# A first partition maximum on POOL, head-norm roots spread through memory, plain transposes for the first token blocks

## The chip, the cores and the metric

The kernel runs on one core of one Trainium2 chip. The metric is the time of one execution on the device in microseconds (us), as the median of several runs. One execution is also taken by the hardware profiler; its time is given beside its span, from the first to the last instruction. TensorE (PE in the rows) multiplies matrices, VectorE (DVE) and ScalarE (ACT) work on rows of 128 partitions, POOL (GpSimd) works across partitions, and SP only issues DMAs here.

## The reference

One decoder block on 1024 tokens of width 1024, in float32. Two branches run side by side, a gated linear recurrence (HGRN2, 8 heads of 128) and sliding-window attention with sinks (16 query heads of 64):

```python
xn = rms_norm(x, norm_w[l])
proj = xn @ w_in[l]
hq, hf, hi, hg, aq, ak, av, ag, mh, ma = jnp.split(proj, SPLIT_POINTS, axis=-1)
f = lb + (1.0 - lb) * sigmoid(hf);  k_h = 1.0 - f;  q_h = silu(hq);  v_h = hi
o_h = hgrn2_chunkwise(q_h, k_h, v_h, log(f))
o_h = rms_norm(o_h, hgrn_norm_w[l])          # one norm per head and token
y_h = (o_h * silu(hg)) @ w_branch_hgrn[l]
y_a = (attention(aq, ak, av, sinks) * silu(ag)) @ w_branch_attn[l]
x = x + (sigmoid(mh) * y_h + sigmoid(ma) * y_a) @ w_out[l]
return rms_norm(x, final_norm_w)
```

## The kernel before

Every product of the large matrices is made of three float16 products: weights and activations are scaled by a power of two and split into a high and a low half (hi, lo). The scale of a weight block comes from its largest absolute value: VectorE reduces along rows (line 205, in the first block line 176), POOL takes the maximum over the partitions (`all_max`, line 122), and a few small VectorE instructions make the power of two (`pow2_of`, lines 125 to 133). ScalarE writes hi, VectorE lo (lines 236 and 237; in the first block, loaded and converted in two parts, lines 194 and 199).

*The front.* `Tokens` loads the eight token blocks of 128 rows. A block's mean square is taken by ScalarE (`square`, lines 427 and 428, with a square root), and `diag` refines the inverse root in four small VectorE instructions. For blocks 0 to 3 it then writes the identity, scaled by that root, into `dg` (line 454), and `turn_x` (line 460) turns and scales a 128x128 piece by a float32 matmul with `dg`, which TensorE runs as two instructions. Blocks 4 to 7 are scaled whole (line 450) and turned by a plain transpose with the identity (line 458), one instruction a piece. `split_x` (lines 464 and 465) multiplies by the norm's gains and writes the halves xh (ScalarE) and xl (VectorE). `norm_w` arrives as 8 rows on SP's queue and is turned by TensorE with the identity (line 150); its maximum (line 344) gives the scale of x. The identity comes from a POOL memset and an affine_select (masks.py:199). TensorE is kept busy beforehand by 24 transposes of the identity (line 1123). All this stands in a stretch with an order written by hand (`tc.manual_schedule`, from line 1119): there each engine's queue follows the program text. Outside it, the build's own scheduler orders each engine's instructions.

*The blocks.* Each block of `seq` is 256 columns of a weight; TensorE goes through the blocks one after the other, into accumulator banks from a pool of three (`pj`). The recurrence of each head (`hgrn`) is a generator that runs in the background: `bg.step(ns)` is called after each part of a block and lets the generators run on a credit of `bg.rate` (half) of the ns that TensorE spends, each `yield cost, wait` taking `cost` from the credit and barring that head for `wait` ns. Ahead of the last head gate, `bg.drain()` emits what is left.

*The head norm.* `o` (tile kT) is a head's output with the value dimension on the partitions and 1024 tokens along the row, `k` holds its squares. TensorE sums the squares over partitions (`ms`, line 681), so that the mean squares, and after `rsqrt` the inverse roots `rs`, stand as 128 partitions by 8 columns: token t of chunk c at partition t, column c. They are needed along the row and equal on all partitions. Two groups of four float32 matmuls (`rb`, line 690) with the identity spread them, and VectorE multiplies each half of `o` by them (line 694).

Of the kernel before, what the change touches and what calls it, by code (L numbers as in the profile page):

```python
# [14 lines left out]
F32 = mybir.dt.float32  # L15
# [4 lines left out]
ALU = mybir.AluOpType  # L20
# [3 lines left out]
P = 128  # L24
# [43 lines left out]
def hybrid_block(ctx: ExitStack, tc: _tile.TileContext, x, norm_w, w_in, hlb, hnw, wbh, sinks, wba, w_out, fnw, out):  # L68
# [9 lines left out]

    uid = [0]
# [55 lines left out]

    ident = const.tile([P, P], F32, name="ident")
# [4 lines left out]
    nwr = slot("nwr", [KT, P])  # L141
    SP.dma_start(nwr[:], norm_w[0].rearrange("(k p) -> k p", p=P))
# [5 lines left out]
    def turn_rows(src, n):  # L148
        ps = bank("vT")
        PE.transpose(ps[:, 0:n], src[:], ident[0:n, 0:n])  # L150
        return ps
# [190 lines left out]
    def norm_max():  # L342
        nmx = small("nmx", 1)
        V.tensor_reduce(nmx[:], nw[:], axis=AX.X, op=ALU.max, apply_absolute_value=True)
        return all_max(nmx[:])

    def norm_scale(top):
        sx, sxi = pow2_of(top, 10)
        yield
        V.tensor_copy(sxi_c[:], sxi[:])  # L350
        V.tensor_scalar(nws[:], nw[:], sx[:], None, ALU.mult)
# [62 lines left out]
    class Tokens:  # L414
# [22 lines left out]
        def diag(self, scaled=False):  # L437
            r, h = self.r, self.h
            V.reciprocal(r[:], r[:])
            if self.by_act:  # L440
                V.tensor_scalar(h[:], self.m[:], EPS, -0.5, ALU.add, ALU.mult)
            else:
                V.tensor_scalar(h[:], self.m[:], -0.5, None, ALU.mult)
            yield
            V.scalar_tensor_tensor(h[:], r[:], h[:], r[:], ALU.mult, ALU.mult)
            yield
            V.scalar_tensor_tensor(r[:], h[:], 1.5, r[:], ALU.add, ALU.mult)
            yield
            if scaled:
                V.tensor_scalar(self.x[:], self.x[:], r[:], None, ALU.mult)  # L450
                self.dg = None
                return
            self.dg = slot("dg", [P, P])
            V.tensor_scalar(self.dg[:], ident[:], r[:], None, ALU.mult)

    def turn_x(ps, tok, j, k):
        if tok.dg is None:
            PE.transpose(ps[:, j * P : (j + 1) * P], tok.x[:, k * P : (k + 1) * P], ident[:])
            return
        PE.matmul(ps[:, j * P : (j + 1) * P], tok.x[:, k * P : (k + 1) * P], tok.dg[:], start=True, stop=True)  # L460
# [74 lines left out]
    def hgrn(h):  # L535
# [148 lines left out]
        rsqrt(rs[:], rm[:], NB)  # L684
        yield 1800, 8000
        for b in range(2):
            rb = bank("rb")
            for j in range(4):
                p = 4 * b + j
                PE.matmul(  # L690
                    rb[:, j * P : (j + 1) * P], rs[:, p : p + 1].broadcast_to([P, P]), ident[:], start=True, stop=True
                )
            sli = slice(b * HALF, (b + 1) * HALF)
            V.tensor_tensor(o[:, sli], o[:, sli], rb[:], ALU.mult)
            if b == 0:
                yield 900, 0
# [422 lines left out]
    with tc.manual_schedule(engines=MANUAL):  # L1119
        A.activation(small("tab", 1)[:], eps[:], AF.Sqrt)  # L1120
        warm = bank("warm", pj)
        for i in range(WARM):
            PE.transpose(warm[:, 0:P], ident[:], ident[:])
            if i == 3:
                V.tensor_copy(nw[:], turn_rows(nwr, KT)[:, 0:KT])
# [20 lines left out]
        in_turn(norm_scale(top))  # L1146
        first.max_part(0)
        tok[0].square(True)
        tok[1].square(True)
        first.scale_part(0)  # L1150
        first.hi_part(0, 0)
        in_turn(tok[0].diag())
        tok[2].square(True)
        in_turn(tok[1].diag())
# [3 lines left out]
        in_turn(tok[2].diag())  # L1158
        in_turn(tok[3].diag())
# [26 lines left out]
        bounds = turn_rows(vecs, 3 * KT)  # L1186
# [10 lines left out]
        in_turn(tok[4].diag(True), tok[5].diag(True))  # L1197
        in_turn(tok[6].diag(True), tok[7].diag(True))
# [142 lines left out]
```

## Time and profile before

| | before |
|---|---|
| median of 3 runs | 1202.01 us (1199.67 to 1202.31) |
| the profiled execution | 1200.46 us |
| its span | 1198.8 us |
| TensorE (PE) busy | 1150.4 us (96%) |
| VectorE (DVE) busy | 860.6 us (72%) |
| ScalarE (ACT) busy | 527.1 us (44%) |
| POOL busy | 46.3 us (4%) |
| DMA, mean | 69 GB/s |
| TensorE clock granted, mean | 0.991 |

The page's 40 slices of 30 us show TensorE at three tenths in the first slice, and at nine tenths or more in nearly all that follow, so the busy share of the whole says little of the front. A busy TensorE is not one at its peak. In a timeline row, "x8" means eight instructions that were merged; the start is that of the first. [...]

### The profile page before, as it was taken

To read this page: it belongs to the slowest core of one execution; us is meant where nothing else is said; L and a number is where in the kernel's file an instruction comes from. 1 tells how busy PE (TensorE), PEld (TensorE's weight loads), DVE (VectorE), ACT (ScalarE), POOL (GpSimd) and SP (SyncE) were. 2 spreads that over 40 slices of the span, in tenths; PEclk is the share of its full clock that TensorE was granted. 3 is DMA by queue.
4 is the path that set the end of the run, shared out by engine and by line. 5 is a ranking of instruction groups with operands and counts; after the bars stand their busy time and mean duration, and the time that the engine had idled before them with its cause. 6 is when DMAs were issued, how large, how long until landed. Compare 5 with 4: busy or idle time off the path is not lost.

```text
span 1198.8 us, 18078 instructions
## 1 busy us (share of the span) xinstructions
PE 1150.4 (96%) x7130; PEld 671.7 (56%) x7130; DVE 860.6 (72%) x2032; ACT 527.1 (44%) x1021; POOL 46.3 (4%) x96
## 2 busy tenths in 40 slices
PE   3999999999999999999999989999997999999997
PEld 3556687687688576574554544445454444444444
DVE  2887886895995996775777774259996877367645
ACT  2732532533433343353845761147778450223323
POOL 0240000000000000000000000000000000000000
PEclk8999999999999999999999999999999999999999
DMA  6121111111111111112562552124545412131312
GB/s 211 37 98 44 36 36 36 36 36 36 36 36 36 36 36 36 36 36 71 102 128 54 115 115 71 36 71 100 108 95 126 85 36 71 36 106 36 141 53 106
DMA packets 132646, 82.47 MB, mean 69 GB/s; under 512 B 81200, under 2 KB 129360, under 8 KB 132560
## 3 DMA queue, kind: packets, MB, share of 16 engines
q1 hardware_dynamic: 132560, 81.30, 24.7%
q8 instruction: 56, 0.92, 0.3%
q14 instruction: 30, 0.25, 0.1%
HBM read 57.17 MB, written 4.19 MB: 51 GB/s over the span
## 4 chain that ended last, share of the span: by engine, by line
PE 76%; DVE 10%; ACT 6%; DMA 5%; issue 2%; SPq 0%; POOL 0%; DVEq 0%; POOLq 0%; ACTq 0%
PE pm L303 19%; PE pg L303 11%; PE pv L315 7%; PE po L1282 7%; PE pq L303 7%; PE pf L303 5%; PE paq L303 5%; PE lv L613 3%; DMA pT<-ph 3%; ACT sp L816 2%; PE pk L303 2%; DVE ph L827 2%; DMA aot<-ohl 2%; PE pf L1129 1%; DVE sp L806 1%
## 5 line engine op out<-in xcount | busy, mean ns | idle before, releaser
L303 PEld LDWEIGHTS <-wh 128*128 128x128 f16 x2304 | 224.1, 98 | 256.9 <-issue 5.5
L303 PEld LDWEIGHTS <-wl 128*128 128x128 f16 x1152 | 112.7, 98 | 130.2
L236 ACT ACTIVATE wh<-raw,p_s 128x512 f16<-128x512 f32 x164 | 104.6, 709 | 117.3 <-issue 42.7
L237 DVE SCALAR_TENSOR_TENSOR wl<-raw,p_s,wh 128x512 f16<-128x512 f32 x164 | 114.1, 748 | 45.1 <-PE pm L303 18.6
L205 DVE TENSOR_REDUCE wmx<-raw 128x1 f32<-128x2048 f32 x45 | 102.6, 2281 | 47.0 <-DMA raw<-in_w_in_dram 25.2
L303 PE MATMUL pm<-hl,wh 128*128 128x512 f16 x512 | 117.0, 379 | 0.0
L1282 PE MATMUL po<-wo,hl 128*128 128x512 f16 (+1 forms) x408 | 83.1, 367 | 0.0
L816 ACT ACTIVATE sp<-sp,anm 128x256 f32<-128x256 f32 (+1 forms) x128 | 61.7, 483 | 24.5 <-DVE anm L811 24.0
L315 PEld LDWEIGHTS <-xh 128*128 128x128 f16 x640 | 62.7, 98 | 7.7
L1282 PEld LDWEIGHTS <-hl 128*128 128x128 f16 x408 | 39.9, 98 | 43.2
L303 PE MATMUL pg<-xl,wh 128*128 128x512 f16 x256 | 62.0, 379 | 0.0
L303 PE MATMUL pg<-xh,wh 128*128 128x512 f16 x256 | 60.8, 379 | 0.9 <-DVE qs L763 0.9
L303 PE MATMUL pm<-xh,wh 128*128 128x512 f16 x256 | 61.4, 382 | 0.0
L303 PE MATMUL pm<-xl,wh 128*128 128x512 f16 x256 | 61.3, 379 | 0.0
L303 PE MATMUL pg<-xh,wl 128*128 128x512 f16 x256 | 61.1, 379 | 0.0
L303 PE MATMUL pm<-xh,wl 128*128 128x512 f16 x256 | 60.7, 379 | 0.0
L303 PE MATMUL pm<-hl,wl 128*128 128x512 f16 x256 | 60.5, 379 | 0.0
L122 POOL PARTITION_ALL_REDUCE p_r<-wmx x47 | 26.6, 570 | 872.6 <-DVE wmx L205 656.3
L806 DVE CUSTOM_DVE_ANT_0 sp<-as,amask,qsc 128x256 f32<-128x256 f32 (+1 forms) x128 | 52.4, 463 | 3.8 <-DMA pT<-ph 3.5
L497 ACT ACTIVATE sg<-pg,wc 128x512 f32<-128x512 f32 x32 | 21.9, 683 | 47.0 <-PE pg L303 46.9
L315 PE MATMUL pv<-wh,xl 128*128 128x256 f16 x320 | 42.0, 273 | 0.0
L315 PE MATMUL pv<-wh,xh 128*128 128x256 f16 x320 | 41.6, 273 | 0.0
(219 smaller groups left out, 1921.7 us busy)
## 6 DMA issues: line engine op xcount, KB each, us to landing
raw<-in_w_in_dram SPq DMA_DIRECT2D x33, 1024.0 KB, 5.1
xt<-in_x_dram SPq DMA_DIRECT2D x8, 512.0 KB, 6.7
raw<-in_w_branch_hgrn_dram SPq DMA_DIRECT2D x4, 1024.0 KB, 5.2
raw<-in_w_branch_attn_dram SPq DMA_DIRECT2D x4, 1024.0 KB, 5.9
raw<-in_w_out_dram SPq DMA_DIRECT2D x4, 1024.0 KB, 5.1
xr<-in_x_dram SPq DMA_DIRECT2D x8, 512.0 KB, 8.3
out_dram<-xr SPq DMA_DIRECT2D x8, 512.0 KB, 2.6
raw<-in_w_in_dram SPq DMA_DIRECT2D x2, 512.0 KB, 4.1
```

The costliest lines, as they stand in the source:

```text
L122: last_all_max[0] = G.partition_all_reduce(r[:], mx, channels=P, reduce_op=bass_isa.ReduceOp.max)
L205: V.tensor_reduce(mx[:, j : j + 1], self.raw[:, ks], axis=AX.XY, op=ALU.max, apply_absolute_value=True)
L236: A.activation(hi, raw, AF.Copy, scale=s[:])
L237: V.scalar_tensor_tensor(lo, raw, s[:], hi, ALU.mult, ALU.subtract)
L303: PE.matmul(ps, w[:, k, ci * P : (ci + 1) * P], act(ai, k, t0, HALF), start=(n == 0), stop=(n == 3 * KT - 1))
L315: PE.matmul(ps, act(ai, k, t0, P), w[:, k, n0 : n0 + ncol], start=(n == 0), stop=(n == 3 * KT - 1))
L497: A.activation(sg[:], ps[:], AF.Sigmoid, scale=c[:])
L613: PE.matmul(lv[:, ms], kq[:, 0, ms], kq[:, 1, ms], start=True, stop=True)
L806: V.tensor_tensor_reduce(self.s[:, i, 0:nk], self.ps[a][:, e * 256 : e * 256 + nk], amask[:, self.n % 2, 0:nk], qsc[:], NEG, ALU.add, ALU. ...
L816: A.activation(self.s[:, i, 0 : self.nk], self.s[:, i, 0 : self.nk], AF.Exp, bias=self.nm[:, i : i + 1], accum_out=self.dn[:, i : i + 1],)
L827: V.scalar_tensor_tensor(self.hl[:, 1], self.s[:, :, 0 : self.nk], 2.0**14, self.hl[:, 0], ALU.mult, ALU.subtract)
L1282: PE.matmul(ps[:, g[0] : g[1]], mact(ai, k, tb * P, P), w, start=(t == 0), stop=(t == 3 * KT - 1))
```

## The change

Three things are changed.

1. POOL's first instruction of its kind is a maximum over partitions of a column of zeros, ahead of the identity's affine_select; nobody reads the result. `norm_w` is loaded by ScalarE's queue into 8 rows of a tile of 128 rows that VectorE has cleared, and its maximum is taken from there. The turn of `norm_w` moves behind the scaling of token block 0, and the copy out of it into `norm_scale`, which moves behind the first weight part's scale. TensorE's 24 opening instructions become float32 matmuls on a tile of ones.
2. In `hgrn`, the roots `rs` are written by a POOL DMA to 1024 floats in device memory and read back by a second one, broadcast to all 128 partitions, into the tile `k`. One VectorE multiply over 1024 columns, whose second operand steps by 8, replaces two from accumulator banks. The `rb` matmuls are gone. The generator yields once more, 900 of cost.
3. Token blocks 0 to 3 are scaled whole by VectorE and turned by plain transposes, as blocks 4 to 7 were; the scaling of blocks 0 and 1 moves ahead of the weight scale.

```diff
--- before.py
+++ after.py
@@ -76,6 +76,9 @@
     pj = ctx.enter_context(tc.tile_pool(name="pj", bufs=3, space=PSUM))
     sm = ctx.enter_context(tc.tile_pool(name="sm", bufs=5, space=PSUM))
 
+    dr = ctx.enter_context(tc.tile_pool(name="dr", bufs=2, space=bass.MemoryType.DRAM))
+    BQ = nc.gpsimd
+
     uid = [0]
 
     def nm(s):
@@ -133,13 +136,19 @@
         return s, inv
 
 
+    zero = const.tile([P, 1], F32, name="zero")
+    G.memset(zero[:], 0.0)
+    all_max(zero[:])
     ident = const.tile([P, P], F32, name="ident")
     make_identity(nc, ident[:])
     ones = const.tile([P, 1], F32, name="ones")
     G.memset(ones[:], 1.0)
 
-    nwr = slot("nwr", [KT, P])
-    SP.dma_start(nwr[:], norm_w[0].rearrange("(k p) -> k p", p=P))
+    nwr = slot("nwr", [P, P])
+    V.memset(nwr[:], 0.0)
+    A.dma_start(nwr[0:KT, :], norm_w[0].rearrange("(k p) -> k p", p=P))
+    wsrc = slot("wsrc", [P, P])
+    V.memset(wsrc[:], 1.0)
     vecs = slot("vecs", [3 * KT, P])
     nw = const.tile([P, KT], F32, name="nw")
     cols = const.tile([P, 3 * KT], F32, name="cols")
@@ -147,7 +156,7 @@
 
     def turn_rows(src, n):
         ps = bank("vT")
-        PE.transpose(ps[:, 0:n], src[:], ident[0:n, 0:n])
+        PE.transpose(ps[:, 0:n], src, ident[0:n, 0:n])
         return ps
 
 
@@ -341,12 +350,12 @@
 
     def norm_max():
         nmx = small("nmx", 1)
-        V.tensor_reduce(nmx[:], nw[:], axis=AX.X, op=ALU.max, apply_absolute_value=True)
+        V.tensor_reduce(nmx[:], nwr[:], axis=AX.X, op=ALU.max, apply_absolute_value=True)
         return all_max(nmx[:])
 
-    def norm_scale(top):
+    def norm_scale(top, turned):
         sx, sxi = pow2_of(top, 10)
-        yield
+        V.tensor_copy(nw[:], turned[:, 0:KT])
         V.tensor_copy(sxi_c[:], sxi[:])
         V.tensor_scalar(nws[:], nw[:], sx[:], None, ALU.mult)
 
@@ -434,7 +443,7 @@
         def root(self):
             A.activation(self.r[:], self.m[:], AF.Sqrt)
 
-        def diag(self, scaled=False):
+        def scale(self):
             r, h = self.r, self.h
             V.reciprocal(r[:], r[:])
             if self.by_act:
@@ -446,18 +455,10 @@
             yield
             V.scalar_tensor_tensor(r[:], h[:], 1.5, r[:], ALU.add, ALU.mult)
             yield
-            if scaled:
-                V.tensor_scalar(self.x[:], self.x[:], r[:], None, ALU.mult)
-                self.dg = None
-                return
-            self.dg = slot("dg", [P, P])
-            V.tensor_scalar(self.dg[:], ident[:], r[:], None, ALU.mult)
+            V.tensor_scalar(self.x[:], self.x[:], r[:], None, ALU.mult)
 
     def turn_x(ps, tok, j, k):
-        if tok.dg is None:
-            PE.transpose(ps[:, j * P : (j + 1) * P], tok.x[:, k * P : (k + 1) * P], ident[:])
-            return
-        PE.matmul(ps[:, j * P : (j + 1) * P], tok.x[:, k * P : (k + 1) * P], tok.dg[:], start=True, stop=True)
+        PE.transpose(ps[:, j * P : (j + 1) * P], tok.x[:, k * P : (k + 1) * P], ident[:])
 
     def split_x(half, k, ps):
         dst = slice(half * HALF, (half + 1) * HALF)
@@ -682,18 +683,17 @@
         rs, rm = small("ors", NB), small("orm", NB)
         V.tensor_scalar(rm[:], ms[:, 0:NB], EPS, None, ALU.add)
         rsqrt(rs[:], rm[:], NB)
+
+        flatrs = dr.tile([P * NB], F32, tag="rs", name=nm("rsd"))
+        BQ.dma_start(flatrs[:].rearrange("(t c) -> t c", c=NB), rs[:])
+        BQ.dma_start(k[:], flatrs[:].rearrange("(o d) -> o d", o=1).broadcast_to([P, P * NB]))
         yield 1800, 8000
-        for b in range(2):
-            rb = bank("rb")
-            for j in range(4):
-                p = 4 * b + j
-                PE.matmul(
-                    rb[:, j * P : (j + 1) * P], rs[:, p : p + 1].broadcast_to([P, P]), ident[:], start=True, stop=True
-                )
-            sli = slice(b * HALF, (b + 1) * HALF)
-            V.tensor_tensor(o[:, sli], o[:, sli], rb[:], ALU.mult)
-            if b == 0:
-                yield 900, 0
+        yield 900, 0
+        yield 900, 0
+        V.tensor_tensor(
+            o[:].rearrange("p (c t) -> p c t", c=NB), o[:].rearrange("p (c t) -> p c t", c=NB),
+            view(k, 0, [[1, NB], [NB, P]]), ALU.mult,
+        )
         ohT[h] = kT
         ohT_flat[h] = o
         yield 900, 0
@@ -1120,9 +1120,7 @@
         A.activation(small("tab", 1)[:], eps[:], AF.Sqrt)
         warm = bank("warm", pj)
         for i in range(WARM):
-            PE.transpose(warm[:, 0:P], ident[:], ident[:])
-            if i == 3:
-                V.tensor_copy(nw[:], turn_rows(nwr, KT)[:, 0:KT])
+            PE.matmul(warm[:, 0:P], wsrc[:], wsrc[:], start=True, stop=True)
 
         def mm_first(ps, i, half, n, wi, ai, k):
             w = (first.hi, first.lo)[wi]
@@ -1143,20 +1141,21 @@
 
         hf_tiles(0)
         top = norm_max()
-        in_turn(norm_scale(top))
         first.max_part(0)
         tok[0].square(True)
         tok[1].square(True)
+        in_turn(tok[0].scale())
+        turned = turn_rows(nwr[0:KT], KT)
+        in_turn(tok[1].scale())
         first.scale_part(0)
         first.hi_part(0, 0)
-        in_turn(tok[0].diag())
+        norm_scale(top, turned)
         tok[2].square(True)
-        in_turn(tok[1].diag())
+        in_turn(tok[2].scale())
         first.lo_part(0, 0)
         tok[3].square(True)
         first.hi_part(0, 1)
-        in_turn(tok[2].diag())
-        in_turn(tok[3].diag())
+        in_turn(tok[3].scale())
         first.lo_part(0, 1)
         for j in range(4):
             for k in range(6):
@@ -1183,7 +1182,7 @@
         pass_first(ps0, 0, 0, range(KT), (0, 1))
         for i in range(2):
             first.outscale(i)
-        bounds = turn_rows(vecs, 3 * KT)
+        bounds = turn_rows(vecs[:], 3 * KT)
         pass_first(ps0, 0, 1, range(KT), (1, 0))
         pass_first(ps0, 0, 1, range(KT), (0, 1))
         tok[4].square(True)
@@ -1194,8 +1193,8 @@
         V.tensor_tensor(dif[:], l1, l0, ALU.subtract)
         tok[6].square(True)
         tok[7].root()
-        in_turn(tok[4].diag(True), tok[5].diag(True))
-        in_turn(tok[6].diag(True), tok[7].diag(True))
+        in_turn(tok[4].scale(), tok[5].scale())
+        in_turn(tok[6].scale(), tok[7].scale())
         setup_bounds(dif)
         n = [0, 0]
         ps1 = [bank("pf", pj), None]
```

## Rows read from the trace of the kernel before

**Rows 1.** Windows: length, busy PE, PEld, DVE, ACT, POOL, clock, DMA, GB/s.

```profile
60.00:525.00 465.00, 465.00 (x3111) 323.15 (x3110) 372.51 (x731) 175.77 (x305) 25.79 (x43) 1.00 0.13 42
```

**Rows 2.** POOL's timeline: start, duration, instruction, [idle before it, its releaser].

```profile
9.67 0.28 POOL masks.py:199 TENSOR_SCALAR_AFFINE_SELECT ident<-ident 128x128 f32<-128x128 f32 x1 [8.60 <-issue]
18.61 0.38 POOL L122 PARTITION_ALL_REDUCE p_r<-nmx  x1 [8.66 <-issue]
21.23 0.35 POOL L122 PARTITION_ALL_REDUCE p_r<-wmx  x1 [2.25 <-DVE wmx L176]
...
55.97 0.59 POOL L383 TENSOR_SCALAR_AFFINE_SELECT mk<-mk 128x128 f32<-128x128 f32 x1
...
70.55 0.36 POOL L122 PARTITION_ALL_REDUCE p_r<-wmx  x1 [0.80 <-DVE wc L247]
```

**Rows 3.** Timeline of all engines, first 37 us, same columns.

```profile
6.80 1.06 ACT L427 ACTIVATE xj<-xt 128x1024 f32<-128x1024 f32 x1 [4.52 <-DMA xt<-in_x_dram]
...
19.92 1.21 DVE L176 TENSOR_REDUCE wmx<-raw 128x1 f32<-128x1024 f32 x1
...
22.26 0.14 DVE L439 RECIPROCAL xr<-xr 128x1 f32<-128x1 f32 x1
...
22.38 0.72 ACT L194 ACTIVATE wh<-raw,p_s 128x512 f16<-128x512 f32 x1 [12.70 <-DVE p_s L132]
...
22.94 0.29 DVE L454 TENSOR_SCALAR dg<-ident,xr 128x128 f32<-128x128 f32 x1
...
23.28 7.67 PE L460 MATMUL xT<-dg,xt 128*128 128x128 f32 x48 [8.33 <-DVE dg L454]
...
24.03 0.74 DVE L199 SCALAR_TENSOR_TENSOR wl<-raw,p_s,wh 128x512 f16<-128x512 f32 x1
24.17 0.29 ACT L428 ACTIVATE xr<-xm,eps 128x1 f32<-128x1 f32 x1
...
29.86 3.58 ACT L464 ACTIVATE xh<-xT,nws 128x512 f16<-128x512 f32 x6 [3.42 <-PE xT L460]
...
36.34 1.89 PE L1129 MATMUL pf<-xh,wh 128*128 128x512 f16 x8
```

**Rows 4.** VectorE groups by form: count, busy us, mean ns, idle before.

```profile
L694 DVE TENSOR_TENSOR kT<-kT,rb 128x512 f32<-128x512 f32 x16 | 10.9, 681 | 10.2 <-PE rb L690 10.1
L570 DVE TENSOR_TENSOR k<-k,inv 128x256 f32<-128x256 f32 x16 | 10.3, 645 | 0.0
L450 DVE TENSOR_SCALAR xt<-xt,xr 128x1024 f32<-128x1024 f32 x4 | 2.8, 750 | 0.0
```

**Rows 5.** DMA issues, first 60 us: size, median us to landing.

```profile
snk<-in_attn_sinks_dram SPq DMA_DIRECT2D x1, 8.0 KB, 11.4
```

**Rows 6.** Windows of the front, columns as in rows 1.

```profile
12.00:14.00 2.00, 2.00 (x11) 2.00 (x10) 0.00 (x0) 0.00 (x0) 0.00 (x0) 1.00 1.02 403
14.00:14.50 0.50, 0.50 (x7) 0.50 (x6) 0.00 (x0) 0.00 (x0) 0.00 (x0) 1.00 1.04 410
17.00:18.00 1.00, 0.00 (x0) 0.00 (x0) 0.00 (x0) 0.00 (x0) 0.00 (x0) 0.68 1.09 366
27.28:28.28 1.00, 1.00 (x9) 1.00 (x9) 1.00 (x2) 0.00 (x0) 0.00 (x0) 0.84 0.00 0
```

**Rows 7.** Timeline around one group that spreads roots, all engines.

```profile
188.34 1.06 PE L690 MATMUL rb<-ident,ors 128*128 128x128 f32 x8
189.23 1.84 PE L681 MATMUL ms<-ones,k 128*128 128x1 f32 x16
...
193.34 0.17 DVE L112 SCALAR_TENSOR_TENSOR ors<-rq_t,rq_y 128x8 f32<-128x8 f32 x1
```

**Rows 8.** DMA issues, whole execution: count, size, us to landing.

```profile
raw<-in_w_in_dram SPq DMA_DIRECT2D x33, 1024.0 KB, 5.1
...
xr<-in_x_dram SPq DMA_DIRECT2D x8, 512.0 KB, 8.3
out_dram<-xr SPq DMA_DIRECT2D x8, 512.0 KB, 2.6
```

## The prediction

> **What bounds the kernel now.** I read the busy times in long stretches first. From 60 to 525 us TensorE is busy for 465.00 of 465 us, and VectorE, the next engine, for 372.51 [rows 1]: whatever is taken off TensorE there comes off the end, as long as nothing else begins to hold TensorE up, and VectorE has 92 us to spare. The first 60 us are the opposite case; there I read POOL's timeline and then all engines'. POOL idles 8.60 us ahead of its first affine_select (the one that finishes the identity) and 8.66 us ahead of its first partition maximum, with no instruction named as releaser, and never again ahead of either: the select at 55.97 follows a maximum and the maximum at 70.55 follows selects, without such a gap [rows 2]. So these two gaps are the first use of some code, and what was in place after the second gap serves both operations. Everything ahead of the first real matmul hangs on the two gaps in series: the identity turns norm_w, its maximum waits for the second gap and comes at 18.61, VectorE stands in order behind it, so that the first weight maximum reaches POOL at 21.23; the weight scale, the diagonals, the turns from 23.28, and the first split of x at 29.86 follow [rows 2, 3]. After that everything moves with this split.
>
> **The front, part by part.** *POOL's first maximum on a zero column* starts the second kind of load at once. If that code serves the select too, one gap of about 8.6 us is left. It starts, as the first did, near 1.0, so the dummy maximum ends near 10.0, the identity near 10.3. The maximum of norm_w no longer needs the identity: it is taken from the raw rows, padded to 128 partitions. With 0.35 to 0.38 us each [rows 2] the two real maxima end near 10.7 and 11.0, against 21.6 for the second now: 10.6 us earlier. Their inputs are there: the first token block had landed by 6.80 [rows 3], and the first weight half is asked for ahead of it on SP's queue, where it now stands first.
>
> *Chain from 11.0 to the first split.* Weight scale: four small VectorE instructions, 0.8 us as from 21.6 to 22.38; first half of hi on ScalarE 0.72, to 12.6. Token 2: square, read and root, which end at 24.46 now, 1.4 behind that hi, to 13.9; then four small VectorE instructions, 0.7 as from 22.26 to 22.94 [rows 3], and the scaling of the whole block, 0.75 [rows 4], to 15.4. First half of lo 0.74 [rows 3], to 16.1. Token 3's scaling, 0.7 and 0.75, to 17.6 (its square and the second hi lie beside it on ScalarE). With its first turn and the hand-overs between engines, 0.5 in all, the split can start at 18.1, against 29.86. Tokens 0 and 1 are squared from 6.8 to 9.6 and scaled while POOL still loads. TensorE is no longer in this chain: 48 turn instructions in 7.67 us become 24, of which only those of token 3 are left when its block is ready. The scaling of four blocks costs VectorE 0.75 instead of 0.29 each; it is counted in the chain.
>
> That is 11.8 us. Two things take some back. The maximum of the second weight half (1.21 us [rows 3]) lay beside the turns and now follows the last lo on VectorE, so the first lo-split waits for it; the matmuls that run then need only the hi-split, and the second hi starts at about 21.8 either way: 0.4. And TensorE's clock, below. I take 11.0.
>
> What is added here and not seen in the trace is norm_w's load on ScalarE's queue, issued behind VectorE's clearing of the tile. Its landing is bounded by nothing below, and above by the small load of the sinks, which took 11.4 us behind 6 MB in one queue [rows 5]. VectorE's first instruction of the ordered stretch waits for it. Up to a landing at 9 it costs nothing. With an issue at 1.6 and 11.4 us it lands at 13.0, its reduction and that of the weights (1.4 together) reach POOL at 14.4, and 3.7 us of the gain go. It has a queue of its own, so I take no cost. The instruction that turned norm_w moves behind token 0's turn-in and is covered by the wait for token 2.
>
> **The clock in the front.** With the clock column as it stands, transposes alone ran at 11 in 2 us from 12.00 and at 7 in 0.5 us from 14.00: their pace rose after 4 us of nothing else. The column shows the fall to half (0.68 as a mean) at 17, after 2 us of idleness, and full clock again from about 27.6, after 4.3 us of diagonal matmuls [rows 6]. The change warms with 24 matmuls of a ones tile from about 1 us, ends them near 7.5, and idles until 10.3. [...] Hence 0.4 of cost, inside the 11.0. [...]
>
> **The head norms.** Sixteen groups of eight matmul instructions that spread the roots (rb) leave TensorE. One group starts at 188.34 and the next work at 189.23 [rows 7], 0.89 us, so 14.2 us leave the stretch where TensorE never idles. This is the surest term. The weight loads go with them. The two multiplies per head of 0.68 become one over 1024 columns whose second operand steps by eight values. Bounds: the 1.36 of now, and 2.58 for four times a 256-column multiply that steps by four (0.645) [rows 4]; that reading memory in place of the accumulator banks were cheaper, no row says. VectorE's bill rises by 0 to 1.2 us a head, at most 10 us against 92 free. I take the upper end, hidden.
>
> Added per head: POOL issues two DMAs, 4 KB to memory, then 512 KB broadcast into k. The second waits on POOL for the first, and the first for the roots. Queued behind them on POOL are the weight maxima, one per block of weights, which serve the conversion two blocks ahead; a few us of delay there lie under a block of TensorE work. The trace has no POOL DMA. A write of 512 KB landed 2.6 us after its issue, loads of 1 MB and 512 KB after 5.1 and 8.3 [rows 8]; so I bound the round trip by 7.7 and 10.9 us. SP's queue is not passed. By the planner's arithmetic the multiply is emitted at least 11.6 of its us after the sums of squares (1800 + 8000 + 900 + 900 ns of steps), of which the sums and the root take 4.3 (189.23 to 193.51 [rows 7]). That leaves 7.3, and for the first seven heads more, since the credit (half of TensorE's time) is spent on other heads' steps. Only the last head, emitted in the drain ahead of the last head gate, can come short, by 0.4 to 3.6 us of VectorE waiting. Behind that wait stand evacuations, and TensorE has two more banks of 24 matmuls, 5.2 us each. One step of 900 more per head moves the steps of a head behind other work but adds no work. I take 1.0 us for all of this; bounds 0 and 8 (one us of TensorE per head). [...]
>
> **Sum.** 11.0 + 14.2 - 1.0 = 24.2 us. From the profiled execution (1200.46; its span is 1198.8) that gives 1176.3. The median of the runs is 1.55 higher, 1202.01, and what is compared is a median: 1177.8. From 525 us on nothing is changed; for a shift of phases there I allow 2 either way.
>
> **Rivals.** *The identity pays for its own code*: the select loads again behind the dummy maximum, and the real maxima stand behind it on POOL in order. Then they come about 8.5 us later, near 19.5, the split at 26.6, and the front gives 3.3 instead of 11.0: 1185.5. The same follows if the select is still put ahead of the dummy. For it: each operation had one gap of its own. Against it: selects and maxima alternate freely later. Chance 0.10.
>
> [...] Chance 0.07.
>
> *The roots come late* (the other side): POOL fetches code again for each DMA it issues, 8.6 us as in its two gaps. The round trip is then 7.7 + 17.2 = 24.9 us, past the 7.3 of the planner and the 10.4 of two banks by 7.2, and eight heads make 58: 1235, slower. It decides from 3.0 us of TensorE idle per head, a round trip of 20.7; there, with eight times 3.0, the time is 1201.8, no change. Against it: VectorE's queue is ordered outside the first stretch by the build's scheduler, which can put other work ahead of the multiply, and 20.7 is over twice the longest landing. Chances 0.03 slower, 0.02 at no change.
>
> **How the numbers follow.** The forecast has 0.78, with its own range of 1172 to 1183; the rest as given. Faster by over 0.2% (2.4 us, about what a measurement of this kernel tells from no change): 0.95; same 0.02; slower 0.03. The range runs from 1171.5 (12 in the front, no waits, 2 of phase, and the spread of the runs, 2.3) to 1187 (the first rival with 1.5 more of waits).
>
> **What would show it.** One gap of about 8.6 us on POOL, none ahead of the identity; real maxima by 11; the first split (ScalarE, xh) near 18; half clock until about 22. No rb on TensorE, its busy time in the middle about 14 us less and still without idleness; the new multiply waiting for a DMA at most in the last head. Wrong would be: a second gap on POOL, TensorE idle behind pk, pg or pv evacuations, or maxima that wait on POOL behind the roots.

## The result, and the profile after

The changed kernel takes 1179.55 us (median of 4 runs, 1178.85 to 1180.12) against 1201.93 for the kernel before beside it: a ratio of 0.9817, 95% interval 0.9800 to 0.9834. The forecast was 1177.8, in a range of 1171.5 to 1187.0; its sign and its size held. Two of its steps did not. The profiled span is 1177.5 us against 1198.8. TensorE is busy for 1138.9 us instead of 1150.4, VectorE for 870.1 instead of 860.6.

POOL's timeline at the start, after the change (start, duration, engine, line, operation, out<-in; in brackets the idle time before and what ended it), which answers to [rows 2]:

```profile
0.80 0.10 POOL L140 MEMSET zero<- 128x1 f32 x1 [0.29 <-POOLq L1326]
0.83 0.20 POOL masks.py:197 MEMSET ident<- 128x128 f32 x1
1.18 0.35 POOL L125 PARTITION_ALL_REDUCE p_r<-zero  x1
1.48 0.36 POOL masks.py:199 TENSOR_SCALAR_AFFINE_SELECT ident<-ident 128x128 f32<-128x128 f32 x1
3.80 0.35 POOL L125 PARTITION_ALL_REDUCE p_r<-nmx  x1 [1.97 <-DVE nmx L353]
6.56 0.35 POOL L125 PARTITION_ALL_REDUCE p_r<-wmx  x1 [2.41 <-DVE wmx L185]
```

No gap of 8.6 us is left. The two real maxima wait for their inputs alone. The front on VectorE, ScalarE and TensorE, which answers to [rows 3]:

```profile
10.10 0.75 DVE L458 TENSOR_SCALAR xt<-xt,xr 128x1024 f32<-128x1024 f32 x1
10.77 0.15 DVE L132 TENSOR_SCALAR p_r<-p_r 128x1 f32<-128x1 f32 x1
11.53 0.72 ACT L203 ACTIVATE wh<-raw,p_s 128x512 f16<-128x512 f32 x1 [2.16 <-DVE p_r L132]
12.15 1.04 ACT L436 ACTIVATE xj<-xt 128x1024 f32<-128x1024 f32 x1
16.37 0.75 DVE L458 TENSOR_SCALAR xt<-xt,xr 128x1024 f32<-128x1024 f32 x1
17.69 3.58 ACT L465 ACTIVATE xh<-xT,nws 128x512 f16<-128x512 f32 x6 [2.10 <-PE xT L461]
24.13 1.89 PE L1127 MATMUL pf<-xh,wh 128*128 128x512 f16 x8
```

The weight's maximum is there at 6.9, yet its scale (10.77) stands on VectorE behind the scaling of token 1 (10.10), and token 2's square (12.15) on ScalarE behind the first half of hi. The split comes at 17.69 instead of 29.86, the first long run of matmuls at 24.13 instead of 36.34.

To see where the time went, four places serve that both traces have: the first product behind the front (pq), the first product behind the drain (paq), the block behind it (pm), the output product (po). TensorE's timeline of the kernel before, then after:

```profile
59.15 0.59 PE L303 MATMUL pq<-xh,wh 128*128 128x512 f16 x2
517.13 1.04 PE L315 MATMUL pv<-wh,xh 128*128 128x256 f16 x8
539.50 1.89 PE L303 MATMUL paq<-xh,wh 128*128 128x512 f16 x8 [1.25 <-DVE va L743]
560.21 1.89 PE L303 MATMUL pm<-xh,wh 128*128 128x512 f16 x8
1108.54 83.10 PE L1282 MATMUL po<-wo,hl 128*128 128x512 f16 x408
```

```profile
48.30 0.59 PE L312 MATMUL pq<-xh,wh 128*128 128x512 f16 x2
491.80 1.04 PE L324 MATMUL pv<-wh,xh 128*128 128x256 f16 x8
517.46 3.20 PE L312 MATMUL paq<-xh,wh 128*128 128x512 f16 x8 [4.53 <-DVE va L743]
520.45 2.31 PE L312 MATMUL paq<-xl,wh 128*128 128x512 f16 x8
539.86 1.89 PE L312 MATMUL pm<-xh,wh 128*128 128x512 f16 x8
1087.15 83.10 PE L1281 MATMUL po<-wo,hl 128*128 128x512 f16 x408
```

The first queries start 10.85 us earlier. From there to the last block ahead of paq (pv of the attention's values, 517.13 before, 491.80 after) the lead grows by 14.48 to 25.33: the rb matmuls. At paq it is 22.04, at pm 20.35. So 4.98 us were given back around the last head: 3.29 by a longer wait on va, 1.69 because the matmuls behind that wait ran slowly (3.20 and 2.31 us for eight instead of 1.89). The granted clock is at half there (stretch, its length, busy us of PE, PEld, DVE, ACT and POOL, granted clock, DMA share, GB/s; PEld is TensorE's weight load):

```profile
518.00:521.00 3.00, 3.00 (x9) 1.07 (x8) 3.00 (x6) 0.28 (x1) 0.00 (x0) 0.50 0.00 0
```

At po the lead is 21.39.

Why va is late stands in VectorE's and POOL's timelines after the change:

```profile
483.89 0.17 DVE L115 SCALAR_TENSOR_TENSOR ors<-rq_t,rq_y 128x8 f32<-128x8 f32 x1
484.35 0.55 POOL L688 DMA_DIRECT2D rsd<-ors  x1 [23.31 <-DVE ors L115]
486.66 0.55 POOL L689 DMA_DIRECT2D k<-rsd  x1 [1.76 <-DMA rsd<-ors]
490.58 2.04 DVE L693 TENSOR_TENSOR kT<-kT,k 128x1024 f32<-128x1024 f32 x1 [5.86 <-DMA k<-rsd]
```

The last head's roots are ready at 484.06; VectorE then stands still for 5.86 us until they have been through memory. Its gate, its maxima and its split into halves follow in order on VectorE, among other work, and the evacuation va comes behind them, at 516.72.

### The profile page after: what moved, and what is told of

It is laid out like the page before. It is cut to its first block, busy times and chain, and to the rows that moved or that the text cites. A ratio compares the mean times of both kernels' runs of the same rounds, so it can differ in the third digit from the quotient of the medians.

```text
span 1177.5 us, 17842 instructions
## 1 busy us (share of the span) xinstructions
PE 1138.9 (97%) x6994; PEld 657.6 (56%) x6994; DVE 870.1 (74%) x2026; ACT 526.1 (45%) x1021; POOL 53.0 (4%) x114
## 4 chain that ended last, share of the span: by engine, by line
PE 71%; DVE 12%; DMA 8%; ACT 7%; issue 2%; SPq 0%; POOLq 0%; DVEq 0%; ACTq 0%
PE pm L312 19%; PE pg L312 10%; PE pv L324 7%; PE po L1281 7%; PE pq L312 7%; PE pf L312 5%; PE paq L312 5%; DMA pT<-ph 3%; PE lv L614 3%; ACT sp L816 2%; DVE ph L827 2%; DVE wl L246 2%; PE pf L1127 1%; DMA aot<-ohl 1%; DMA raw<-in_w_in_dram 1%
## 5 line engine op out<-in xcount | busy, mean ns | idle before, releaser
L614 PEld LDWEIGHTS lv<-kq 128*128 128x128 f32 x320 | 41.0, 192 | 4.6
L600 ACT ACTIVATE kq<-q 128x512 f32<-128x512 f32 x40 | 25.0, 627 | 39.9 <-DVE q L575 25.4
```

Source lines behind the costliest of these rows:

```text
L600: A.activation(view(kq[:, 1], 0, mdims), view(q, c, qdims), AF.Copy)
L614: PE.matmul(lv[:, ms], kq[:, 0, ms], kq[:, 1, ms], start=True, stop=True)
```

## The experiments

One table first. "Front" is by how much pq starts earlier than in the profiled run of the kernel before (59.15); "head norms" is by how much the stretch from pq to pm is shorter than its 501.06 us; "rest" the same from pm to po (548.33 us). Each is a difference of two starts in TensorE's timeline. Ratios go by the runs of the kernel before on the same chip.

| kernel | median us | ratio (95%) | front | head norms | rest |
|---|---|---|---|---|---|
| changed | 1179.55 | 0.9817 (0.9800 to 0.9834) | 10.85 | 9.50 | 1.04 |
| e4_select_first | 1179.02 | 0.9800 (0.9775 to 0.9825) | 11.95 | 9.72 | -1.54 |
| e1_roots_only | 1193.86 | 0.9927 (0.9903 to 0.9952) | -1.84 | 8.59 | -1.78 |
| e2_front_only | 1188.38 | 0.9883 (0.9859 to 0.9907) | 10.57 | 0.09 | -0.53 |
| e12_max_only | 1186.78 | 0.9880 (0.9864 to 0.9897) | 14.20 | -0.24 | -0.72 |
| e9_max_of_identity | 1191.19 | 0.9920 (0.9901 to 0.9939) | -0.37 | 9.19 | 0.24 |
| e3_last_rb | 1176.93 | 0.9787 (0.9765 to 0.9809) | 12.19 | 13.09 | -1.88 |
| e5_no_extra_step | 1176.48 | 0.9802 (0.9785 to 0.9818) | 10.77 | 12.80 | 0.06 |
| e8_step_one | 1178.61 | (one run) | 10.62 | 12.34 | -0.94 |
| e6_front_order | 1177.77 | 0.9810 (0.9787 to 0.9833) | 14.65 | 8.72 | -0.63 |
| e7_no_warm | 1184.72 | 0.9872 (0.9855 to 0.9888) | 10.74 | 8.68 | -4.70 |
| e11_warm_one | 1184.78 | 0.9864 (0.9849 to 0.9879) | 11.93 | 9.08 | -4.56 |
| e10_both_orders | 1175.80 | 0.9794 (0.9776 to 0.9812) | 12.90 | 12.47 | -0.92 |

The last column shows how far to trust a microsecond: no kernel was edited behind pm, and but for e7 and e11 it lies between -1.9 and 1.0. The front column holds a chance of its own. The traces of the changed kernel, e2, e5, e7 and e8 show TensorE at half clock for a few us from about 37 us on (0.50 in the changed kernel, where a matmul of 512 columns takes 0.63 us instead of 0.38; the same 0.63 in the others), and fronts of 10.57 to 10.85; those of e3, e4 and e11, with the same orders on VectorE, ScalarE and POOL in the front, show full clock there (0.38) and 11.93 to 12.19. In e10 the fall comes at about 35 us (0.63 at 35.65) and in e9, 11 us later like its whole front, at about 48 (0.63 at 48.66); e6 and e12 have none (1.00 from 36 to 40 us in e12). e4 is the same program as the changed kernel, so this fall, worth 1.1 to 1.4 us, belongs to the one execution and not to the kernel.

### The two halves of the change, apart

e1: the kernel before with the change's `hgrn` (memory roots) alone. e2: the changed kernel with this undone:

```diff
-        BQ.dma_start(flatrs[:].rearrange("(t c) -> t c", c=NB), rs[:])
-        BQ.dma_start(k[:], flatrs[:].rearrange("(o d) -> o d", o=1).broadcast_to([P, P * NB]))
...
+                PE.matmul(
+                    rb[:, j * P : (j + 1) * P], rs[:, p : p + 1].broadcast_to([P, P]), ident[:], start=True, stop=True
+                )
```

> The kernel before with the head norms' roots through memory and nothing else of the change. The theory read from the two traces: sixteen groups of eight rb matmuls leave TensorE (16 x 0.89 = 14.2 us; the block starts showed 14.5 us between 194 and 496 us), and the last head's norm, which ends after the matmuls that could cover it, gives back 4 to 5 us, of which about 1 us is regained later: 1191 to 1193 us, 9 to 11 us under the kernel before, with paq waiting about 4.5 us for va. Rival: the loss at the last head belongs to the earlier start that the front gives, not to the trip through memory: 1187 to 1188 us, paq waiting about 1.2 us.

> The changed kernel with the head norms' roots spread by rb matmuls as before; the front of the change alone. Theory: the 10.85 us by which the block starts lie earlier at the first queries go through to the end, 1190.5 to 1191.5 us, and paq waits for va as little as before (about 1.2 us). Rival: the earlier start leaves the last head's norm uncovered by itself; paq waits 4 to 5 us and the time is 1194 to 1196 us.

e1 comes to 1193.86, e2 to 1188.38. The two halves give 7.2 and 12.7 us against the 1201.04 beside them, 19.8 together, where the whole change gave 22.0 on the same chip (e4, below). From pq to the last block ahead of paq e1 is 14.48 us shorter (60.99 to 504.49), to the hundredth what the changed kernel is, and e2 0.00. TensorE then waits 5.2 us for va in e1, and in e2 1.2 us for a converted weight and none for va: the loss at the last head belongs to the trip through memory, as the theory has it, and not to the earlier start. Both medians missed their theory's range. e1 ends 0.9 us above it; in its profiled run, the slowest of the four (1195.68), the front was 1.84 later (TensorE waits 9.4 us for the first diagonal there, not 8.3). e2 ends 2.1 us below it, with a front as early as expected in the profiled run (1190.34, also the slowest of its four); what made the others faster was not traced.

### What the front's gain hangs on

Three kernels bear on the order on POOL. e4 puts `all_max(zero[:])` behind `make_identity`; in e9 the maximum also needs the select's result (its edit is shown); e12 is the kernel before with the maximum of zeros and nothing else.

```diff
-    zero = const.tile([P, 1], F32, name="zero")
-    G.memset(zero[:], 0.0)
-    all_max(zero[:])
     ident = const.tile([P, P], F32, name="ident")
     make_identity(nc, ident[:])
+    all_max(ident[:, 0:1])
```

> The changed kernel with the order of the first two POOL operations turned round: the identity's select ahead of the maximum over partitions of zeros. Theory: what the engine holds of code at the start is the maximum's, and the code loaded at its first need by the select's side costs a gap; with select first two gaps of 8.6 us return, as in the kernel before, the real maxima come at about 18 to 21 us and the time rises by 5 to 9 us, to 1185 to 1188 us. Rival 1: one load serves both operations and is needed once whatever the order; as the changed kernel shows none, this one shows none either, and the time is 1179 to 1180 us. Rival 2: one gap of 8.6 us, ahead of the select alone: identity and zeros' maximum at about 10 us, the real maxima right behind, time 1180 to 1184 us.

In e4 the build's scheduler put the maximum first again, so that its instructions are those of the changed kernel. It says nothing on the order; it is a second measurement of the same program (1179.02 beside 1179.55), whose trace differs by 1.1 us at pq and 2.6 us between pm and po.

> The changed kernel, where the first maximum over partitions takes a column of the identity instead of zeros, so that it must follow the identity's select (its result is used by nothing, as before). Theory: the instruction list then has a load of POOL's code ahead of the select and another ahead of the maximum, as in the kernel before; each of them costs what it did there, 8.6 us, and the real maxima come at about 18.6 and 21 us instead of 3.8 and 6.6; the identity comes at about 9.7 us and lets the tokens be turned meanwhile, so that about half of the front's gain stays: 1183 to 1188 us. Rival: what cost 8.6 us twice in the kernel before was not the order of the two operations but something else that the change removed (the ten DMA issues on SP ahead of the first); then POOL shows no gap here, and the time is 1179 to 1180 us.

POOL in e9, where the order is forced:

```profile
0.97 0.10 POOL L347 MEMSET eps<- 128x1 f32 x1
10.21 0.58 POOL masks.py:199 TENSOR_SCALAR_AFFINE_SELECT ident<-ident 128x128 f32<-128x128 f32 x1 [9.14 <-issue]
20.61 0.38 POOL L125 PARTITION_ALL_REDUCE p_r<-ident  x1 [9.82 <-issue]
20.90 0.42 POOL L125 PARTITION_ALL_REDUCE p_r<-nmx  x1
21.23 0.42 POOL L125 PARTITION_ALL_REDUCE p_r<-wmx  x1
```

Both gaps are back, 9.14 and 9.82 us, with everything else of the change in place, and the front's gain is gone (59.52 at pq against 59.15). So the order of the two operations makes the gaps, not the queue that was relieved. The time, 1191.19, was a miss: half of the gain was to stay. It did not, since the tokens could not be turned meanwhile: TensorE's waits name one of 11.4 us on nw, whose copy out of its bank stands on VectorE behind the weight's scale, which needs the maximum at 21.23.

> The kernel before with one thing of the change: the maximum over partitions of zeros at the start of POOL's work. Theory: both gaps of 8.6 us go, because the maximum's code then serves the select too and is there from the start; the identity comes at about 1.5 us, the real maxima at about 4 to 7 us, and most of the front's 10.85 us comes with that alone: the first split at 18 to 21 us, 1189.5 to 1193 us. Rival: the gaps go, but the diagonal matmuls and the queue of the norm weights' load behind the warm-up keep the front late, so that less than half of it comes: 1195 to 1198 us.

POOL, ScalarE and TensorE in e12:

```profile
1.17 0.35 POOL L122 PARTITION_ALL_REDUCE p_r<-zero  x1
3.70 0.35 POOL L122 PARTITION_ALL_REDUCE p_r<-nmx  x1 [1.87 <-DVE nmx L347]
9.49 7.25 PE L463 MATMUL xT<-dg,xt 128*128 128x128 f32 x48 [2.04 <-DVE dg L457]
9.69 0.71 ACT L197 ACTIVATE wh<-raw,p_s 128x512 f16<-128x512 f32 x1
15.66 3.58 ACT L467 ACTIVATE xh<-xT,nws 128x512 f16<-128x512 f32 x6 [1.92 <-PE xT L463]
44.95 0.59 PE L306 MATMUL pq<-xh,wh 128*128 128x512 f16 x2
```

The maximum of zeros alone brings 14.20 us at pq, more than the whole front of the change (10.85, or 11.95 in e4's trace of the same program), and 1186.78 us beside e2's 1188.38. That is better than its theory had it (a split at 18 to 21 us, 1189.5 to 1193). A diagonal takes VectorE 0.29 us where the scaling of a token takes 0.75 [rows 3, 4]; hi starts at 9.69 instead of 11.53 and the split at 15.66 instead of 17.69, although TensorE still runs 48 turn instructions for 7.25 us. So the plain transposes and the new order took back some 2 us by the split and by the first long run (22.15 instead of 24.13); the rest of the 3.35 us at pq is the fall of the clock near 37 us that e12's trace does not have. In the medians of e2 and e12 the difference is not resolved.

e6 keeps the plain transposes and changes the order: all four squares ahead, the weight's scale ahead of the tokens' scalings, its hi and lo behind them.

```diff
-        tok[0].square(True)
-        tok[1].square(True)
+        for t in tok[:4]:
+            t.square(True)
+        first.scale_part(0)
...
```

> The changed kernel with another order of the first stage's emission: all four squares first, the first weight's scale ahead of the tokens' scales, its hi and lo parts behind them. Theory: the first split at 17.7 us is now set by the order on ScalarE and VectorE, in which token 2's and 3's squares stand behind the weight's hi and lo parts; with the squares ahead the split starts at about 14.1 us and the time is 3 us less, 1176 to 1177 us. Rival: the split waits for the tokens' arrival or the weight's hi part instead, and the front stays within 1 us of where it is: 1178.5 to 1180 us.

The split starts at 15.08, 2.6 us ahead of the changed kernel, and the first long run of matmuls at 21.92, 2.2 ahead: the order was what bound the front. pq, at 44.50, is 3.8 us ahead, but 1.4 of that is the fall of the clock near 37 us, which this trace does not have. The time lies between the ranges of theory and rival: the median falls by 1.8 (1177.77), and by the ratios, 0.9810 and 0.9817, the gain is not resolved; the profiled run loses 0.8 at the last head and 1.7 behind it.

### The last head

```diff
+        if h == NH - 1:
+            ...
+                    rb[:, j * P : (j + 1) * P], rs[:, p : p + 1].broadcast_to([P, P]), ident[:], start=True, stop=True
```

> The changed kernel, where the last head alone spreads its roots by rb matmuls on TensorE; the other seven go through memory. Theory: the round trip through memory of the last head (about 6 us between the roots and the multiply) is what paq waits for; the wait on va falls from 4.5 to about 1.2 us and TensorE's clock stays up behind it: 1174.5 to 1176.5 us. Rival: what is late is the order that the emission gives the last head's steps in the drain, whatever spreads the roots: 1178.5 to 1180.5 us.

e5 takes one `yield 900, 0` out of the head norm, so that the planner counts it as before.

> The changed kernel with one step of 900 fewer in the head norms' cost list, so that the planner counts a head norm as in the kernel before. Theory: the last head's norm is late because the planner's budget no longer reaches its end before the drain, and then its trip through memory is uncovered; with the step gone the norm is emitted earlier, paq's wait on va falls from 4.5 to below 2 us, and the time is 1176 to 1178 us. Rival: the round trip alone makes the wait, wherever the planner puts the steps: paq waits 4 to 5 us, 1179 to 1180 us.

TensorE's waits on va (us in total, times, longest), in e3, then in e5:

```profile
PE paq L312 <- DVE va L757: 0.8, 1, 0.8
```

```profile
PE paq L312 <- DVE va L742: 0.9, 1, 0.9
```

Both mend it: the stretch pq to pm is 13.09 and 12.80 us shorter than before, instead of 9.50. In e5 the last head's roots leave POOL at 470.54 instead of 484.35; TensorE has two waits elsewhere that the changed kernel has not (on kk and p_u, 0.7 us each). So the loss needs both: a trip of 6 us and a planner that, with one step more per head, emits this head's norm some 14 us later. Take either away and it is gone. The medians fall by less than the traces at pm, to 1176.93 (0.4 us above e3's range) and 1176.48 (inside e5's), and the intervals of the ratios overlap the changed kernel's. In e3 most of the difference (4.93 us ahead of the changed kernel at pm, 1.8 behind this place) goes at the next place where TensorE waits for VectorE; there the changed kernel, which arrives later, loses less. TensorE's row at that place in the changed kernel and in e3:

```profile
610.04 1.90 PE L312 MATMUL paq<-xh,wh 128*128 128x512 f16 x8 [1.23 <-DVE qs L763]
```

```profile
606.73 3.38 PE L312 MATMUL paq<-xh,wh 128*128 128x512 f16 x8 [1.96 <-DVE qs L777]
```

### The multiply

```diff
-            view(k, 0, [[1, NB], [NB, P]]), ALU.mult,
+            view(k, 0, [[P, NB], [1, P]]), ALU.mult,
```

> The changed kernel, where the head norms' multiply reads the roots in the order in which they lie (step 1) instead of with a step of 8 elements; it so multiplies tokens with the wrong roots, which changes no cost but the reading. Theory: the 2.02 us of the multiply come from the step; with step 1 it takes 1.2 to 1.4 us, and the time is unchanged within 1 us, since VectorE is not what bounds that stretch. Rival: the multiply takes 2.02 us for its three-dimensional view of 1024 columns whatever the step.

The group of the multiply (count, busy us, mean ns, idle ahead) in the changed kernel, then with step 1:

```profile
L693 DVE TENSOR_TENSOR kT<-kT,k 128x1024 f32<-128x1024 f32 x8 | 16.2, 2024 | 16.3 <-DMA k<-rsd 16.3
```

```profile
L693 DVE TENSOR_TENSOR kT<-kT,k 128x1024 f32<-128x1024 f32 x8 | 9.7, 1218 | 16.3 <-DMA k<-rsd 16.3
```

The step of 8 elements costs 0.81 us of the 2.02. The time is unchanged within a microsecond, as expected. In this one trace the last head came off 2.8 us better (12.34 for 9.50; paq waits 3.4 us and its matmuls run at full speed).

### The warm-up

e7 sets `WARM = 0`, e11 `WARM = 1`.

> The changed kernel without the 24 warm-up matmuls. Theory: TensorE's clock falls to half at 14 us in the changed kernel, warm-up or not, and is full again from about 19.4 us by the turns and the first pass themselves, so that the warm-up does nothing: 1179 to 1180 us, and the same granted clock from 16 us. Rival: the warm-up still keeps the first turns at full clock and without it the front ends 1 to 2 us later: 1180.5 to 1181.5 us.

> The changed kernel with one warm-up matmul instead of 24; the bank of the warm-up is taken as before. Without any warm-up matmul the front was as early as in the changed kernel, but 5.7 us were lost behind 540 us. Theory: that loss came from the bank that nothing then held, which moved the later banks' turn, and not from the clock; with the bank taken the time is 1178.5 to 1180.5 us. Rival: the warm-up itself is worth it, through the clock of the stalls; the time is 1184 to 1186 us again.

1184.72 and 1184.78: the warm-up is worth some 5 us, and both theories of e7 fall with that, for the front is as early without it (pq at 48.41 and 47.22). The loss lies between pm and po (-4.70 and -4.56), at the attention's waits for VectorE and for turned DMAs, 550 us behind the edit. e11 rules out the bank. Its rival has the time right; whether it has the reason is not shown. Of the 5.7 and 5.6 us that e7 and e11 lose on the changed kernel between pm and po, 3.7 and 3.8 go at one place, where that kernel waits 1.23 us for qs and runs on at full clock (its row at 610.04 above). They wait longer there, first for a turned DMA and then 2.0 and 2.2 us for qs, and the matmuls behind the wait are slow, e7's and then e11's:

```profile
613.28 3.08 PE L312 MATMUL paq<-xh,wh 128*128 128x512 f16 x8 [2.03 <-DVE qs L763]
```

```profile
611.57 2.96 PE L312 MATMUL paq<-xh,wh 128*128 128x512 f16 x8 [2.19 <-DVE qs L763]
```

e3, which has the warm-up, shows the same at the same place (606.73), so a missing warm-up is not needed for it. The mean granted clock decides nothing here: it is 0.991 and 0.994 against 0.990, but leaves out the slow start of e7 (last section). The order of the instructions is otherwise the same. What carries the loss so far stays open.

### Both edits that helped

> The changed kernel with both edits that helped alone: the head norms' step of 900 taken out and the squares of the first four tokens ahead in the first stage. Theory: the gains add, 3.8 us earlier at the first queries and about 2 to 3 us at the last head, of which the later attention stalls take back half: 1174 to 1176.5 us. Rival: those stalls take back all of the second gain: 1176.5 to 1178 us.

1175.80, inside the theory's range and the fastest kernel of this study, 3.8 us under the changed one by the medians, though the intervals of the ratios overlap. It holds the last head's gain (12.47). Of e6's front it shows 12.90 of 14.65: its split starts only 0.3 us later (15.37), and the rest is a fall of the clock to half at about 35 us, which e6's trace has not. e12's front with e5's head norms was not run.

## Why the prediction was right, and where it was not

*POOL: wrong, and it hardly mattered.* "One gap of about 8.6 us is left" was the failed step; there is none. That what is in place for the first maximum serves the select too was right: the select runs 0.3 us behind it (1.48 and 1.18), and e9 shows both gaps again, 9.14 and 9.82 us, as soon as the select is first. What was missed is that the maximum, put first, shows no gap at the start, while the select does (8.60 us before). The built instruction lists of POOL differ in just this: before, and in e9, a load of code stands ahead of the select and another ahead of the first maximum; after, and in e12, a single one stands ahead of the maximum of zeros. That the gaps are these loads is the author's inference from this match; the rows of the gaps, 8.60 to 9.82 us long, name nothing in them. In the kernel before they lie beside a busy DMA (a share of 0.96 to 1.17 from 5 to 18 us). Why the maximum shows no gap where it comes first is open; no run tested it.

*The front: right in size, by two errors that met.* The maxima came at 3.8 and 6.6, not at 10.7 and 11.0, but the chain did not start there: tokens land at 6.5 and VectorE's order puts the weight's scale at 10.77, so hi ended at 12.25 against the 12.6 that was reckoned, and the split came at 17.69 against 18.1. The gain was 12.2 us at the long matmuls (24.13 against 36.34), so the 0.8 set aside for the first fall of the clock and for the second maximum did not show. Then a second fall of the clock, not foreseen, took 1.36 of it. The changed kernel at that place, then e4, the same program:

```profile
36.00:37.00 1.00, 0.00 (x0) 0.00 (x0) 0.00 (x0) 1.00 (x2) 0.00 (x0) 0.79 0.00 0
37.00:40.00 3.00, 2.79 (x9) 1.56 (x9) 2.81 (x2) 1.35 (x4) 0.00 (x0) 0.50 0.00 0
```

```profile
37.00:40.00 3.00, 2.52 (x16) 1.65 (x16) 2.54 (x2) 2.27 (x4) 0.00 (x0) 1.00 0.00 0
```

(Columns as at the last head above.) TensorE had idled 1.45 us there; the kernel before idles as long at its own such place (ahead of 49.42) and shows 1.00. Hence 10.85 for the 11.0, and 11.95 in e4: that the front came within 0.2 us of its term is luck. The landing of norm_w, taken at no cost, was at 3.42.

*The first fall of the clock.* Half clock was expected until about 22 us; it shows from 12.7 to 19.5 (0.85 as the mean of 12 to 13 us, 0.50 of 13 to 14, 0.74 of 19 to 20). No run shows the 0.4 us that the sum holds for it: the lead is 12.17 us at the split and 12.21 at the long matmuls. The matmuls of 512 columns take 0.63 us at 18.51 and 0.38 from 19.66, 1.1 us into the first pass and behind 12 transposes. What the transposes and what the matmuls had in this rise, the row does not separate.

*The head norms: right.* 14.2 reckoned, 14.48 measured, in e1 too, with TensorE busy throughout. POOL issued each DMA in 0.55 to 0.73 us, and no gap of some 8 us without a releaser stands ahead of one, so the rival of the late roots is out. The multiply took 2.02 us, inside 1.36 to 2.58.

*The allowance: the right place, the wrong size.* 1.0 us was taken for waits, with bounds 0 and 8; 4.98 went. The last head, in the drain, was named. Its trip was shorter than its bounds (6.2 us from the first issue to the multiply, against 7.7 to 10.9), but VectorE waited 5.86 us, more than the 3.6 reckoned, because the planner's distance of 7.3 us did not exist: between the roots and the wait VectorE had 0.66 us of other work. The sign "waiting for a DMA at most in the last head" failed with it: VectorE waited at four of the eight multiplies (6.72, 1.16, 2.58 and 5.86 us), though only the last wait reached TensorE. The cover of "two more banks, 5.2 us each" was no cover, since everything up to va stands on VectorE behind the multiply. And 1.69 us were the slow matmuls behind TensorE's wait, which no term held. Of the 4.98, 1.04 came back behind pm, less than the 2.6 by which two traces of this program (the changed kernel's and e4's) differ there.

In all: 10.85 + 14.48 - 4.98 + 1.04 = 21.39 us by po, where 24.2 was reckoned.

## What to carry to other kernels

Look for idle time that no releaser explains ahead of an engine's first instructions of a kind, and try another order of them: here it was 8.60 and 8.66 us on POOL, and one instruction of 0.35 us whose result nobody reads, put first, was worth 14 us, and the rest of the redesigned front, in the order it was given, nothing that the medians show. When a step is moved to a slower path, price it at the last iteration, where a planner's slack has run out, and add the clock that TensorE can lose by the wait: 1.7 us here behind 4.5 us, nothing behind the 3.4 us of e8. Where two traces differ by a microsecond, compare their clock columns before naming a cause. A gain ahead of a stretch with waits of its own can come through in part alone: of e3's 4.93 us at pm, 1.8 were left behind the next wait.

## What the hardware showed that was not expected

*The clock column does not tell the pace at the start of a trace.* In e7, without the warm-up, the column shows 1.00 from 18 to 20 us, while a matmul of 512 columns takes 0.63 us, as at the 0.50 of the changed kernel (18.51), until 19.65 and 0.38 from 20.01:

```profile
18.00:20.00 2.00, 2.00 (x7) 0.89 (x6) 2.00 (x3) 2.00 (x5) 0.35 (x1) 1.00 0.70 208
```

```profile
19.22 0.63 PE L1127 MATMUL pf<-xh,wh 128*128 128x512 f16 x1
20.01 0.38 PE L1127 MATMUL pf<-xh,wh 128*128 128x512 f16 x1
```

The column shows 1.00 where the trace has no record of the clock. The first record, one of full clock, begins at 5.87 us in the changed kernel and at 13.94 in the kernel before, and the pace rises at just these places: in the changed kernel three of the opening instructions take 0.85 us at 5.05 and 0.50 at 5.89, and in the kernel before a transpose takes 0.42 us until 13.65 and 0.27 from 14.02. So the 1.00 of 12 to 14 us in [rows 6] is no granted clock either, and the rise of the pace that the prediction read there falls together with the first record of full clock. Ahead of the first record, durations have to be read instead.

*VectorE read float32 with a step of 8 elements more slowly here*: 2.02 us against 1.22 for 1024 columns, the other operand and the output unchanged.

*24 matmuls in the first 9 us change the time from 550 us on by some 5 us*, with the order of all other instructions the same. The cause is open.
